# Modulated projection input by two VectorE operations around one ScalarE cast, and group C's attention low parts on GpSimd

## The chip, the cores and the metric

The kernel runs on one core of one Trainium2 chip. The metric is the device time of one execution in microseconds (us). TensorE multiplies matrices, VectorE and GpSimd do elementwise work, ScalarE activations and casts, and SyncE (SP) issues the DMAs.

## The reference

Two layers of a latent-diffusion trunk, on 512 latent tokens and 256 context tokens of width 1024. Each layer normalizes and modulates its input, projects it, lets three head groups attend, gates them, projects back and adds the residual:

```
sh, sc, gt = split(silu(c) @ w_ada[l] + b_ada[l], 3)
h  = rms_norm(x, norm_g[l]) * (1 + sc) + sh            # hc for the context tokens alike
qa, ka, va, ga, qb, kb, vb, gb, qn, kn, vn, gn = split_proj(h @ w_in[l])
# A: differential attention with rotary, B: grouped-query attention with rotary,
# C: 8 x 16 neighbourhood attention with a learned bias; each also attends to the context
y  = concatenate([ya, yb, yn]) @ w_out[l]              # each group gated by silu of ga, gb, gn
x  = x + gt * y                                        # the context likewise in the first layer
```

The first step's `rms_norm(...) * (1 + sc) + sh` is what the change touches: with rs the reciprocal root mean square of a token, mA = norm_g (1 + sc) and mB = sh, it is h = x rs mA + mB.

## The kernel before

Tokens lie along the free dimension: a tile of x is 128 features by 512 latents (`bigL`) or by 256 context tokens (`bigC`), and there are 8 feature tiles (kt 0 to 7). Products that need fp32 accuracy are made from two parts, hi (a value cast to fp32r) and lo (the value less its hi), by three matmuls: xh whi (L685), xh wlo (L686), xl whi (L687). `build_h` makes hi and lo of h for one kt and one stream. It is called 32 times, 8 kt by 2 streams by 2 layers:

- L431, VectorE: xn = x rs (rs is broadcast over partitions in the tile `stB`). xn is a tile of a ring of three (`p32`, printed as p).
- L432, VectorE: xn = xn mA + mB, with mA and mB as one number per partition.
- L434, ScalarE: hi = cast of xn.
- L435: lo = xn - hi, on VectorE for kt 0, 3 and 6, on GpSimd for the others.

In layer 0, `proj_first` takes kt after kt for all six token tiles of the first weight chunk (6 x 3 matmuls of 384 columns per kt), and before each kt it calls `ada_pair`, which makes mA and mB of that kt: matmuls with the modulation weights (L198) into a PSUM tile of a ring of two, a VectorE copy (L201), a summing matmul (L203), and two small VectorE operations that write mA (L208) and mB (L211). The layer's constants (`layer_consts`, L310 to L382, many tiny VectorE and GpSimd operations) are made in the same stretch. The weights' own low parts (`wlo`, L85) are made on GpSimd ahead of that stage and on VectorE during the first chunks. In layer 1 the context's h is built first, behind the sums of squares over the new x (L1190, summed by matmuls L400), then the latents' h.

The order of the instructions on each engine is planned at build time, from priorities and a model of the engines' times; each engine then runs its list in order.

In attention, a unit is one head by 128 queries: scores (L781), maximum (L836, or L833 with the bias table of group C), ScalarE exponential (L850) into a tile of the same `p32` ring, a cast to fp16 hi (L870), the low part p - hi (L871), a DMA that transposes both (L873), and the value matmuls (L906, L907). The engine of L871 is chosen by a table of shares,

```python
VSHARE = {"HA": (0, 1), "H": (0, 1), "G": (1, 1), "T": (1, 4), "HC": (1, 8), ...}
```

where "H" is the low part, the letter behind it the group, and (a, b) gives VectorE a of every b. Group A and B give all to GpSimd; group C gives every eighth to VectorE.

Of the kernel before, what the change touches and what calls it, by code (L numbers as in the profile page):

```python
# [10 lines left out]
F32 = mybir.dt.float32  # L11
# [4 lines left out]
AF = mybir.ActivationFunctionType  # L16
ALU = mybir.AluOpType
# [17 lines left out]

REST = {"C": 7}
AK = [[6, 2, 0, 2], [0, 1, 0, 2]]
VSHARE = {"HA": (0, 1), "H": (0, 1), "G": (1, 1), "T": (1, 4), "HC": (1, 8), "WB": (1, 2), "WC": (1, 1),
          "W1": (1, 1)}

class Share:
# [5 lines left out]
    def __call__(self, kind):  # L47
        a, b = VSHARE.get(kind + self.phase, VSHARE.get(kind, (0, 1)))
        i = self.n[kind] = self.n.get(kind, -1) + 1
        return self.nc.vector if i * a % b < a else self.nc.gpsimd  # L50
# [59 lines left out]
def tile_hybrid_block(ctx: ExitStack, tc: tile.TileContext, xT_d, cT_d, ng_d, w_ada, bT_d, w_in, w_out,  # L110
# [7 lines left out]
    V, A, G, PE, SP = nc.vector, nc.scalar, nc.gpsimd, nc.tensor, nc.sync  # L118
# [3 lines left out]
    def sb(shape, dt=F32, tag="", bufs=1):  # L122
        return pool.tile(shape, dt, tag=tag, bufs=bufs, name=tag)
# [38 lines left out]
    def big(s, dt=F32, shape=None):  # L162
        return sb(shape or [128, KT, SW[s]], dt, "bigL" if s == 0 else "bigC", 3)
# [247 lines left out]
    def norm_both():  # L411
        acc = nbuf["t"][:, 0:NT]
        rs = nbuf["t"][:, NT:2 * NT]
        ps = psV.tile([128, 512], F32, tag="pv", name="ssq")
        for j in range(6):
            PE.matmul(ps[:, j:j + 1], lhsT=acc[:, 128 * j:128 * j + 128], rhs=colD, start=True, stop=True)
        r = rsqrt(ps[:, 0:6], 6, 1.0, EPS)
        for st_, js in ((0, range(4)), (1, range(4, 6))):
            ps = psP.tile([128, 512], F32, tag="p", name="rsb")
            for i, j in enumerate(js):  # L420
                PE.matmul(ps[:, 128 * i:128 * i + 128], lhsT=r[:, j:j + 1].to_broadcast([128, 128]), rhs=ident,
                          start=True, stop=True)
            A.copy(out=rs[:, 128 * js[0]:128 * js[-1] + 128], in_=ps[:, 0:128 * len(js)])
        return rs[:, 0:NL], rs[:, NL:NT]

    def build_h(l, st_, kt, x, rs):
        mA, mB, _ = mods[l]
        w = SW[st_]
        hi, lo = hT[st_]
        xn = sb([128, NT], F32, "p32", 3)[:, 0:w]  # L430
        V.tensor_tensor(out=xn, in0=x[:, kt, :], in1=rs, op=ALU.mult)  # L431
        V.tensor_scalar(out=xn, in0=xn, scalar1=mA[:, kt, st_:st_ + 1], scalar2=mB[:, kt, st_:st_ + 1], op0=ALU.mult,  # L432
                        op1=ALU.add)
        A.copy(out=hi[:, kt, :], in_=xn)  # L434
        (V if kt % 3 == 0 else G).tensor_tensor(out=lo[:, kt, :], in0=xn, in1=hi[:, kt, :].bitcast(F32),  # L435
                                                 op=ALU.subtract)


    NH = {"A": 8, "B": 6, "C": 6}
# [759 lines left out]
    if True:  # L1199
        cT = sb([128, KT, 2], F32, "cT")  # L1200
        SP.dma_start(out=cT, in_=cT_d)
        x = [big(0), big(1)]
# [29 lines left out]
        rs = norm_both()  # L1232
# [3 lines left out]
        def before0(gi, kt):  # L1236
            if kt:
                ada_pair(ada0[kt])
            for st_ in range(2):
                build_h(0, st_, kt, x[st_], rs[st_])  # L1240
            if kt == 5:
                layer_consts(0)
# [7 lines left out]
        for l in range(DEPTH):  # L1250
# [14 lines left out]
            x = [big(0), big(1)]  # L1265
            open_norm()
            rs = [None, None]
# [6 lines left out]
            for kt in range(KT):  # L1274
                prio(-800)(build_h)(l + 1, 1, kt, x[1], rs[1])

            def before1(gi, kt):
                if gi == 1:
                    if kt == 0:
                        rs[0] = norm_finish(0)  # L1280
                        hT[0] = (big(0, F32R), big(0, F32R))
                    prio(-800)(build_h)(1, 0, kt, x[0], rs[0])
# [79 lines left out]
```

## Time and profile before

| | before |
|---|---|
| runs, median of 3 (lowest to highest) | 934.97 us (934.93 to 936.88) |
| the profiled execution | 930.04 us |
| its span in the profile | 928.2 us |
| mean granted TensorE clock | 0.95 |
| busy share: TensorE, VectorE, ScalarE, GpSimd | 89%, 74%, 64%, 58% |
| L431, L432, both streams, 64 instructions | 45.1 us busy |
| L434, 32 instructions | 15.9 us busy |
| L435, 20 on GpSimd, 12 on VectorE | 23.8 us on GpSimd |
| L871, 138 on GpSimd, 6 on VectorE | 204.2 us and 6.3 us |

Busy times are sums over instructions of the profiled execution; successive VectorE instructions overlap by under 0.1 us, so that sums are a little high. "PE" is TensorE's matmul, "PEld" its weight load, "DVE" VectorE, "ACT" ScalarE, "POOL" GpSimd, "SPq" the DMA issue of SyncE. A row of the timeline is start, duration, engine, line, operation, output and inputs, shape; in brackets stands how long the engine was idle before and what released it.

### The profile page before, as it was taken

The numbers are of one execution on the slowest core, as the hardware profiler recorded it, in microseconds if no ns is written. First come the engines' busy times: TensorE is split into PE (matmuls) and PEld (weight loads), VectorE is DVE, ScalarE is ACT, GpSimd is POOL, SyncE is SP. The second block draws the span as 40 slices with busy tenths as digits, with TensorE's granted clock in tenths as the row PEclk, the third lists the DMA queues.
The fourth block names the chain that finished last, engine by engine and source line by source line (L and its number), as shares of the span: only waits on it lengthen the run. The fifth ranks groups of instructions, "written<-read, shape, count | busy, mean of one in ns | idle before, by whom it ended". The sixth has DMA issues, their size and how long they took to land.

```text
span 928.2 us, 17966 instructions
## 1 busy us (share of the span) xinstructions
PE 829.5 (89%) x6386; PEld 709.7 (76%) x6386; DVE 682.7 (74%) x1306; ACT 592.3 (64%) x1269; POOL 541.3 (58%) x502
## 2 busy tenths in 40 slices
PE   5899997997998999797999989989959999988978
PEld 3788886786887889685777889878849888866757
DVE  5975788988678866467765797789877975855853
ACT  5334577885887687476563445478758978757740
POOL 2638846998798465432441047939988776732420
PEclk9899999998999999899999999999979999987979
DMA  9925895644979997989898713884556889995642
GB/s 307 331 90 135 204 215 133 154 85 127 194 156 221 195 221 170 227 213 229 183 234 235 243 61 101 184 189 101 140 132 156 168 188 249 240 253 134 134 114 83
DMA packets 361449, 165.47 MB, mean 178 GB/s; under 512 B 256656, under 2 KB 355216, under 8 KB 361104
## 3 DMA queue, kind: packets, MB, share of 16 engines
q1 hardware_dynamic: 361360, 164.33, 73.9%
q8 instruction: 50, 0.82, 0.4%
q14 instruction: 39, 0.32, 0.1%
HBM read 86.55 MB, written 15.47 MB: 110 GB/s over the span
## 4 chain that ended last, share of the span: by engine, by line
PE 46%; DVE 15%; DMA 13%; POOL 9%; issue 8%; ACT 7%; SPq 1%; DVEq 0%; POOLq 0%; ACTq 0%
PE proj L685 7%; PE proj L687 7%; PE proj L686 6%; PE sc L781 5%; DMA pt<-hl 4%; PE pv L906 3%; PE op L1093 3%; PE op L1094 3%; PE op L1095 2%; ACT p L850 2%; DVE mx L836 2%; DMA raw<-in_w_in_dram 2%; DMA stB<-in_btab_dram 2%; POOL hl L871 2%; POOL wlo L85 1%
## 5 line engine op out<-in xcount | busy, mean ns | idle before, releaser
L871 POOL TENSOR_TENSOR hl<-p,hl 128x768 f16<-128x768 f32 (+3 forms) x138 | 204.2, 1484 | 179.7 <-ACT hl L870 139.7
L685 PE MATMUL proj<-whi,bigL 128*128 128x384 f32 (+1 forms) x592 | 203.4, 344 | 9.8 <-DVE tb L608 3.8
L686 PE MATMUL proj<-wlo,bigL 128*128 128x384 f32 (+1 forms) x592 | 200.3, 338 | 0.9 <-POOL wlo L85 0.7
L687 PE MATMUL proj<-whi,bigL 128*128 128x384 f32 (+1 forms) x592 | 197.7, 336 | 0.0
L850 ACT ACTIVATE p<-sc,nb,gsc 128x768 f32<-128x768 f32 (+3 forms) x200 | 166.0, 844 | 14.3 <-DVE p L866 5.0
L836 DVE TENSOR_REDUCE mx<-sc 128x1 f32<-128x768 f32 (+2 forms) x128 | 118.7, 931 | 31.7 <-PE sc L781 31.2
L685 PEld LDWEIGHTS proj<-whi,bigL 128*128 128x128 f32 x592 | 115.4, 195 | 19.9 <-DVE tb L608 5.4
L870 ACT CAST hl<-p 128x768 f16<-128x768 f32 (+3 forms) x144 | 103.7, 725 | 33.0 <-DMA pt<-hl 18.5
L686 PEld LDWEIGHTS proj<-wlo,bigL 128*128 128x128 f32 x592 | 115.5, 195 | 3.9 <-POOL wlo L85 1.6
L687 PEld LDWEIGHTS proj<-whi,bigL 128*128 128x128 f32 x592 | 114.4, 194 | 3.3 <-issue 2.4
L85 POOL TENSOR_TENSOR wlo<-raw,whi 128x768 fp32r<-128x768 f32 (+1 forms) x44 | 82.9, 1893 | 30.0 <-ACT whi L82 24.8
L82 ACT CAST whi<-raw 128x768 fp32r<-128x768 f32 (+1 forms) x104 | 80.3, 779 | 30.8 <-DMA raw<-in_w_in_dram 16.2
L906 PEld LDWEIGHTS <-pt 128*128 128x128 f16 x736 | 65.9, 99 | 41.2 <-DMA pt<-hl 25.7
L85 DVE TENSOR_TENSOR wlo<-raw,whi 128x768 fp32r<-128x768 f32 (+1 forms) x60 | 65.2, 1090 | 25.3 <-ACT whi L82 22.5
L685 PE MATMUL proj<-whi,bigC 128*128 128x384 f32 (+2 forms) x224 | 75.8, 339 | 0.8 <-ACT xn L468 0.8
L686 PE MATMUL proj<-wlo,bigC 128*128 128x384 f32 (+2 forms) x224 | 74.8, 334 | 0.0
L687 PE MATMUL proj<-whi,bigC 128*128 128x384 f32 (+2 forms) x224 | 74.6, 335 | 0.0
L156 POOL TENSOR_TENSOR rsqb<-rsqb,half 128x12 f32<-128x12 f32 (+2 forms) x25 | 68.2, 2726 | 10.5 <-DVE rsqb L155 8.4
L907 PEld LDWEIGHTS <-pt 128*128 128x128 f16 x736 | 66.6, 100 | 4.2 <-issue 1.2
L906 PE MATMUL pv<-vA,pt 128*128 128x128 f16 (+2 forms) x424 | 52.2, 229 | 13.6 <-DMA pt<-hl 13.0
L838 ACT ACTIVATE nb<-mx,lnp,gsc 128x1 f32<-128x1 f32 (+1 forms) x104 | 39.6, 385 | 37.6 <-DVE mx L836 26.5
L781 PE MATMUL sc<-bigL 128*128 128x512 f16 (+4 forms) x184 | 46.1, 310 | 17.3 <-ACT p L850 16.7
(320 smaller groups left out, 2042.2 us busy)
## 6 DMA issues: line engine op xcount, KB each, us to landing
raw<-in_w_in_dram SPq DMA_DIRECT2D x56, 384.0 KB, 4.1
adw<-in_w_ada_dram SPq DMA_DIRECT2D x68, 256.0 KB, 3.8
raw<-in_w_in_dram SPq DMA_DIRECT2D x24, 256.0 KB, 3.6
raw<-in_w_out_dram SPq DMA_DIRECT2D x16, 384.0 KB, 4.0
g_d<-tb SPq DMA_DIRECT2D x20, 192.0 KB, 2.6
gt<-g_d SPq DMA_DIRECT2D x18, 192.0 KB, 2.9
hl<-in_w_ada_dram SPq DMA_DIRECT2D x12, 256.0 KB, 5.0
pt<-in_w_ada_dram SPq DMA_DIRECT2D x12, 256.0 KB, 5.2
```

The lines of the kernel that those rows point to most:

```text
L82: self.nc.scalar.copy(out=hi, in_=raw2)
L85: self.share("W").tensor_tensor(out=lo, in0=raw2, in1=hi.bitcast(F32), op=ALU.subtract)
L156: G.tensor_tensor(out=y, in0=x, in1=half[:, 0:n], op=ALU.pow)
L685: PE.matmul(ps, lhsT=xh, rhs=hi, start=(kt == 0), stop=False)
L686: PE.matmul(ps, lhsT=xh, rhs=lo, start=False, stop=False)
L687: PE.matmul(ps, lhsT=xl, rhs=hi, start=False, stop=(kt == KT - 1))
L781: PE.matmul(ps, lhsT=q, rhs=k, start=n == 0, stop=n == b[2] - 1)
L836: V.tensor_reduce(out=mx[:, 0:ns], in_=ps[:, 0:w * ns].rearrange("p (a b) -> p a b", b=w), axis=AX.X, op=ALU.max)
L850: A.activation(out=p[:, w * x:w * x + w], in_=u["ps", i][:, w * x:w * x + w], func=AF.Exp, bias=u["nb", i][:, x:x + 1], scale=lc[l]["sc"][ ...
L870: A.copy(out=hl[:, 0:n], in_=p)
L871: lo_eng.tensor_tensor(out=hl[:, n:2 * n], in0=p, in1=hl[:, 0:n], op=ALU.subtract)
L906: PE.matmul(po[r, :], lhsT=pt[:, b, r], rhs=V_[:, vt, c0:129], start=first, stop=False)
```

## The change

`build_h` does L431 and L432's work by one VectorE scalar_tensor_tensor, xn = x mA rs, without the shift. The ScalarE cast becomes an Identity activation with mB as its bias, so that hi = cast of (xn + mB). The low part is a second scalar_tensor_tensor, lo = (xn + mB) - hi, on VectorE for every kt. In the table of shares the entry "HC" goes, so that group C's L871 falls under "H" and is on GpSimd always.

```diff
-VSHARE = {"HA": (0, 1), "H": (0, 1), "G": (1, 1), "T": (1, 4), "HC": (1, 8), "WB": (1, 2), "WC": (1, 1),
+VSHARE = {"HA": (0, 1), "H": (0, 1), "G": (1, 1), "T": (1, 4), "WB": (1, 2), "WC": (1, 1),
           "W1": (1, 1)}
...
         xn = sb([128, NT], F32, "p32", 3)[:, 0:w]
-        V.tensor_tensor(out=xn, in0=x[:, kt, :], in1=rs, op=ALU.mult)
-        V.tensor_scalar(out=xn, in0=xn, scalar1=mA[:, kt, st_:st_ + 1], scalar2=mB[:, kt, st_:st_ + 1], op0=ALU.mult,
-                        op1=ALU.add)
-        A.copy(out=hi[:, kt, :], in_=xn)
-        (V if kt % 3 == 0 else G).tensor_tensor(out=lo[:, kt, :], in0=xn, in1=hi[:, kt, :].bitcast(F32),
-                                                 op=ALU.subtract)
+        V.scalar_tensor_tensor(out=xn, in0=x[:, kt, :], scalar=mA[:, kt, st_:st_ + 1], in1=rs, op0=ALU.mult,
+                               op1=ALU.mult)
+        b = mB[:, kt, st_:st_ + 1]
+        A.activation(out=hi[:, kt, :], in_=xn, func=AF.Identity, bias=b)
+        V.scalar_tensor_tensor(out=lo[:, kt, :], in0=xn, scalar=b, in1=hi[:, kt, :].bitcast(F32), op0=ALU.add,
+                               op1=ALU.subtract)
```

## The prediction

> **What bounds the kernel now.** I read the first and fourth parts of the page, then the table by stretches over the two places where the input is built, then the single instructions there. TensorE is busy 89% of the span, VectorE 74%, GpSimd 58%.
>
> ```profile
> span 928.2 us, 17966 instructions
> ...
> PE 829.5 (89%) x6386; PEld 709.7 (76%) x6386; DVE 682.7 (74%) x1306; ACT 592.3 (64%) x1269; POOL 541.3 (58%) x502
> ```
>
> `build_h` runs only between about 20 and 65 us (layer 0) and between 535 and 565 us (layer 1). In the table by stretches the columns are TensorE, its weight load, VectorE, ScalarE and GpSimd (busy us, instructions), the granted clock, the DMA share and GB/s:
>
> ```profile
> 20.00:30.00 10.00, 8.75 (x84) 6.76 (x77) 10.00 (x16) 4.52 (x11) 5.78 (x4) 0.83 1.12 337
> 30.00:40.00 10.00, 7.43 (x86) 6.12 (x85) 9.35 (x44) 2.81 (x9) 7.52 (x15) 0.85 1.10 327
> 40.00:50.00 10.00, 10.00 (x94) 8.66 (x94) 9.96 (x19) 3.73 (x9) 4.27 (x3) 0.98 1.04 311
> ...
> 540.00:550.00 10.00, 10.00 (x66) 9.39 (x64) 9.09 (x18) 4.28 (x11) 4.74 (x6) 0.89 0.00 0
> 550.00:560.00 10.00, 10.00 (x66) 9.85 (x58) 9.96 (x16) 5.03 (x13) 6.34 (x6) 1.00 0.19 54
> ```
>
> VectorE is full in all of these, and TensorE is full in three of the five. So a relief of VectorE is paid only where TensorE stands still or is slow; these places are the terms of the sum. They are, after the VectorE row that releases the first:
>
> ```profile
> 36.56 0.21 DVE L211 TENSOR_SCALAR mB<-ada,bT 128x2 f32<-128x2 f32 x1
> 36.87 0.56 PE L198 MATMUL ada<-hl,cS 128*32 128x128 f32 x8 [2.57 <-issue]
> 39.13 0.52 PE L686 MATMUL proj<-wlo,bigL 128*128 128x384 f32 x1
> 39.45 0.52 PE L685 MATMUL proj<-whi,bigL 128*128 128x384 f32 x1
> ...
> 60.31 0.44 PE L685 MATMUL proj<-whi,bigL 128*128 128x384 f32 x1 [0.78 <-ACT bigL L434]
> 60.59 0.34 PE L686 MATMUL proj<-wlo,bigL 128*128 128x384 f32 x1
> 60.76 0.34 PE L685 MATMUL proj<-whi,bigL 128*128 128x384 f32 x1
> ...
> 537.18 1.05 PE L400 MATMUL ssq<-colD,stB 128*128 128x1 f32 x8 [3.64 <-DVE stB L1190]
> 564.60 0.44 PE L687 MATMUL projs<-whi,bigL 128*128 128x384 f32 x1 [0.66 <-POOL bigL L435]
> ```
>
> After the 2.57 us gap a 384-column matmul starts every 0.32 us (39.13 to 39.45); after the 0.78 us gap, every 0.17 us (60.59 to 60.76). A long gap is thus paid a second time in a halved clock, a short one is not.
>
> **The change part by part.** Per call `build_h` had a VectorE multiply by rs (L431), a VectorE scale-and-shift (L432), a ScalarE cast (L434) and a subtraction (L435), on VectorE for kt 0, 3 and 6 and on GpSimd for the other five. Now it has two VectorE scalar_tensor_tensor around a ScalarE Identity with a bias. There are 8 calls per stream and layer, 32 in all. The durations (min/median/max, ns):
>
> ```profile
> L431 DVE TENSOR_TENSOR p<-bigL,stB x16: 675/687/2247, 19.8 to 560.4; 128x512 f32<-128x512 f32 x16
> L431 DVE TENSOR_TENSOR p<-bigC,stB x16: 410/420/2051, 20.5 to 543.2; 128x256 f32<-128x256 f32 x16
> ...
> L432 DVE TENSOR_SCALAR p<-p,mA,mB x32: 393/539/1750, 21.4 to 561.7; 128x512 f32<-128x512 f32 x16, 128x256 f32<-128x256 f32 x16
> ...
> L435 POOL TENSOR_TENSOR bigL<-p,bigL x10: 1291/1454/2242, 26.0 to 564.5; 128x512 fp32r<-128x512 f32 x10
> L435 POOL TENSOR_TENSOR bigC<-p,bigC x10: 731/744/982, 29.5 to 545.2; 128x256 fp32r<-128x256 f32 x10
> L435 DVE TENSOR_TENSOR bigL<-p,bigL x6: 675/680/689, 24.2 to 561.1; 128x512 fp32r<-128x512 f32 x6
> L435 DVE TENSOR_TENSOR bigC<-p,bigC x6: 410/419/426, 25.2 to 544.6; 128x256 fp32r<-128x256 f32 x6
> ```
>
> L432's row mixes the sizes: I read its median 539 as the undisturbed 512-wide pass and its minimum 393 as the 256-wide one. The new instruction at these sizes stands elsewhere in the kernel, with one input from PSUM; it will cost between L431's 0.687 and 0.420, which reads two SBUF tensors too, and these rows, which I take because the operation is the same:
>
> ```profile
> L1136 DVE SCALAR_TENSOR_TENSOR bigC<-op,mG,hl x4: 481/484/484, 509.0 to 515.7; 128x256 f32<-128x256 f32 x4
> L1136 DVE SCALAR_TENSOR_TENSOR bigL<-op,mG,pt x4: 745/748/751, 517.8 to 531.7; 128x512 f32<-128x512 f32 x4
> ```
>
> VectorE, undisturbed, per kt with both streams: before 0.687 + 0.420 for L431, 0.54 + 0.39 for L432, and in three of eight cases 0.680 + 0.419: 2.04 + 0.41 = 2.45 us on average. After: 2 x (0.748 + 0.484) = 2.46 us. VectorE's own work does not move: the change trades a cheap pass for the return of the GpSimd share. GpSimd loses 10 x 1.454 + 10 x 0.744 = 22 us of medians, all off the end's path except where it is named below.
>
> What moves is that GpSimd leaves the build. Its instruction stretches the VectorE one beside it:
>
> ```profile
> 26.03 1.71 POOL L435 TENSOR_TENSOR bigL<-p,bigL 128x512 fp32r<-128x512 f32 x1 [2.25 <-ACT bigL L434]
> 26.50 1.39 DVE L432 TENSOR_SCALAR p<-p,mA,mB 128x256 f32<-128x256 f32 x1
> ```
>
> The 256-wide L432 took 1.39 us, ending just after the GpSimd one at 27.74; its minimum is 0.393, so it lost 1.0 us. The new instructions read two SBUF tensors as L431 does, whose maximum of 2051 to 2247 ns shows that it suffers alike; so they will be stretched by what stays on GpSimd (the weight splits of L85), but not by L435. The Trainium skill (GPSIMD Engine Reference, Specifications) says that GpSimd shares its SBUF interfaces with VectorE and collides with instructions in a two-port mode or with two SBUF inputs; by that rule old and new forms are equally exposed, and the trace agrees (1.39 against 0.393 us).
>
> Term A, the 2.57 us gap. The third pair's shift (L211) was written at 36.56 to 36.77, and TensorE's next modulation matmuls, which reuse that PSUM tile, followed at 36.87. VectorE worked without a hole from 19.85 to there, so what it sheds ahead of this point closes the gap. kt 0 (whose subtraction was on VectorE): 3.14 to 2.46, -0.7. kt 1: 2.04 to 2.46, +0.4. The stretch at 26.50: -1.0. kt 2's two multiplications (0.687 + 0.420) could run ahead of their modulation factors; the new form multiplies by mA first and cannot, so -1.1 here. Together -2.4. I count 2.0 of the 2.57 and half of the clock's second price. That price: 8 matmuls at 0.32 instead of 0.17 are 1.2 us, of which 0.6. Bounds of A: a loss of 1.2, if the order on VectorE leaves the layer constants ahead of L211 and adds kt 1's two low parts (0.748 + 0.484), and a gain of 2.57 + 1.2 = 3.8.
>
> Term B, the 0.78 us gap at 60.31. One kt earlier the multiplication had to wait for a buffer of xn (a ring of three), held by a GpSimd subtraction:
>
> ```profile
> 57.29 0.94 DVE L431 TENSOR_TENSOR p<-bigC,stB 128x256 f32<-128x256 f32 x1 [0.86 <-POOL bigL L435]
> ```
>
> With the subtraction at 0.748 on VectorE right behind the cast, it comes free some 1.3 us earlier: gain 0.7 (bounds 0 and 0.8). Term C, 537.18: the first hi of layer 1 needs one VectorE pass of 0.484 instead of 0.420 + 0.393, 0.33 sooner, and the passes around the last sums of squares become fewer: 0.7 (bounds 0 and 2.0; the gap is mostly the last sum of squares itself). Term D, 564.60: the GpSimd low part was late; gain 0.6 (bounds 0 and 0.66). Behind 538 us TensorE is full, so the rest of layer 1's build is worth nothing: 30 us of TensorE cover it, and if that cover went, VectorE's 2.46 us per kt would still be under the 6 x 3 matmuls x 0.17 = 3.1 us of a kt.
>
> ScalarE: the cast gains a bias read from memory.
>
> ```profile
> L434 ACT CAST bigL<-p 128x512 fp32r<-128x512 f32 x16 | 9.6, 619 | 24.5 <-DVE p L432 24.4
> ...
> L850 ACT ACTIVATE p<-sc,nb,gsc 128x512 f32<-128x512 f32 x36 | 26.8, 770 | 4.8 <-DVE hl L871 2.8 <-POOL hl L871 1.7
> ```
>
> A 512-wide activation with two such operands takes 770 against 619 ns, so one costs between 0 and 0.15; I take 0.08. It is on the path at terms A to C only: -0.2 in all (bounds 0 and -0.4). The Trainium skill (ScalarE: Activation LUTs, What ACT_TABLE_LOAD costs) gives about 93 ns per pointer operand; by that the loss would be 0.3 and the sum 0.1 us smaller. It is a rule against the change.
>
> Group C's low parts: six of L871 go from VectorE to GpSimd. Near the end all three units of a burst are then in one queue:
>
> ```profile
> 883.49 2.34 POOL L871 TENSOR_TENSOR hl<-p,hl 128x512 f16<-128x512 f32 x2 [3.82 <-ACT hl L870]
> 884.98 1.40 DVE L871 TENSOR_TENSOR hl<-p,hl 128x512 f16<-128x512 f32 x1
> 886.41 0.67 ACT L850 ACTIVATE p<-sc,nb,gsc 128x384 f32<-128x384 f32 x1 [0.23 <-DVE hl L871]
> ```
>
> On GpSimd the third ends at 883.49 + 3 x 1.17 = 887.0 instead of 886.4, and the exponential waits for its buffer: +0.6 us; VectorE is free 1.4 us sooner for the next score maximum, which is not late. The other five lie beside output-projection matmuls; all six on the path at 0.55 each would be +3.3, and VectorE's 1.4 us freed at the end, if they count, -1.4. Taken: -0.5, as at the end. No DMA and no queue of SP changes in number; each transposed load of a moved unit is issued up to 0.6 us later.
>
> Sum: 2.6 + 0.7 + 0.7 + 0.6 - 0.2 - 0.5 = 3.9 us. The profiled execution took 930.04 us (928.2 span and 1.8 around it) and would take 926.1; the median of the runs is 934.97, 4.9 above it, so I forecast 934.97 - 3.9 = 931.1.
>
> **Rivals.** (1) Slower: the first pass now needs mA, so nothing of a kt can run ahead of its modulation matmuls. Place: layer 0, kt 1 to 7. After mA comes a 0.748 pass and a 0.70 cast instead of 0.54 and 0.62: 0.29 us per kt, 2.0 us; and with both low parts in VectorE's queue (1.23 us) in front of the next pair's copy and factors, five kts more would lose up to 6.2. With 60% of that, the tail's 0.5 and only terms C and D on the other side: 2.0 + 3.7 + 0.5 - 1.3 = 4.9 us, 939.9. It decides once TensorE waits over 0.7 us for hi or for the factors in five of the seven kts. For it: VectorE at 10.00, 9.35, 9.96 of 10 there. Against: TensorE at 10.00 between 40 and 50 us, fed from behind by low parts of the kt before.
>
> (2) No change: the instructions' order is planned anew at build time from modelled durations, and L211 again stands behind the constants; A and C are 0, B and D stay, the tail and the bias cost 0.6: 934.97 - 1.3 + 0.6 = 934.3.
>
> (3) Slower by the tail: GpSimd's bursts put all six moved parts on the path, +3.3, the bias 0.2, and A and C bring nothing: 934.97 + 3.5 - 1.3 = 937.2. For it: L850 waits for the VectorE part already (0.23 above). Against: five of the six have matmuls of the output projection beside them.
>
> (4) More than forecast: A entire (3.8), B and D entire, C 2.0 and the clock after its 3.64 us gap (another 1.2), the tail unharmed: 8.5 us, 926.5. For it: a gap of 0.78 us leaves the clock alone, so closing most of a gap saves its second price whole. Against: it asks for four places at once.
>
> **How the numbers follow.** Mine (929 to 933) 0.43, rival 4 0.14, rival 2 0.21, rival 1 0.14, rival 3 0.08. Faster and slower are counted from 0.2%, 1.9 us, about what runs of this kernel can tell from no change: faster 0.57, same 0.21, slower 0.22. The range reaches from half way beyond rival 4, 925.5, to just short of rival 1's value, 938.5; mine alone is 929 to 933.
>
> **What would show it.** L435 absent from GpSimd and no VectorE pass of the build over 1.2 us except beside L85; both passes near 0.74 and 0.48; the gap before TensorE's fifth pair of modulation matmuls under 1 us and 384-column matmuls behind it at 0.17; no gap at the last low part of layer 1. Wrong would be: that gap as long or longer, new waits of L685 for hi in layer 0, or a longer wait of L850 for GpSimd in group C.

## The result and the profile after

The changed kernel takes 943.96 us (median of 4 runs, 942.55 to 946.70) against 934.95 for the kernel before in the same comparison: ratio 1.0099, 95% interval 1.0071 to 1.0128. A second comparison of 12 runs (`e18` below) gave 942.89 us, ratio 1.0059 (1.0031 to 1.0087). The change makes the kernel slower by 0.6 to 1.0%; 931.1 was forecast. The ratios are taken between runs made side by side and need not be the quotients of the medians. The profiled execution took 943.91 us. Its page begins:

```profile
span 942.1 us, 17913 instructions
...
PE 829.7 (88%) x6386; PEld 712.5 (76%) x6386; DVE 667.8 (71%) x1288; ACT 594.7 (63%) x1269; POOL 528.2 (56%) x488
```

TensorE's work is the same (829.5 before), VectorE and GpSimd have less, and the span is 13.9 us longer. The build's instructions, all shapes and durations (min/median/max in ns, first and last start):

```profile
L431 DVE SCALAR_TENSOR_TENSOR p<-bigL,mA,stB x16: 737/746/1217, 20.0 to 560.8; 128x512 f32<-128x512 f32 x16
L431 DVE SCALAR_TENSOR_TENSOR p<-bigC,mA,stB x16: 471/481/2059, 20.7 to 540.7; 128x256 f32<-128x256 f32 x16
L434 ACT ACTIVATE bigL<-p,mB x16: 708/722/727, 20.8 to 562.6; 128x512 fp32r<-128x512 f32 x16
L435 DVE SCALAR_TENSOR_TENSOR bigL<-p,mB,bigL x16: 735/744/752, 21.5 to 564.2; 128x512 fp32r<-128x512 f32 x16
L435 DVE SCALAR_TENSOR_TENSOR bigC<-p,mB,bigC x16: 463/480/2047, 22.2 to 541.9; 128x256 fp32r<-128x256 f32 x16
```

They cost what the prediction took (0.748 and 0.484). The time is lost elsewhere. Five landmarks by their last start, first in before and then in after: the residual of layer 0 (that layer's end), the values of group B (`vB`), group A's gated output (L934), the values of group C (`vnc`), the last residual (L1171). The first start in the first row is the first evacuation of layer 0.

```profile
L592 DVE SCALAR_TENSOR_TENSOR vA<-proj,vna,vA x16: 338/346/353, 69.2 to 595.4; 128x128 f16<-128x128 f32 x16
L1136 DVE SCALAR_TENSOR_TENSOR bigL<-op,mG,hl x4: 745/748/751, 519.9 to 533.6; 128x512 f32<-128x512 f32 x4
L592 DVE SCALAR_TENSOR_TENSOR vB<-proj,vnb,vB x12: 334/340/353, 147.2 to 644.6; 128x128 f16<-128x128 f32 x12
L934 DVE TENSOR_TENSOR o<-o,gt x10: 402/484/1568, 165.0 to 756.2; 128x256 f32<-128x256 f32 x10
L592 DVE SCALAR_TENSOR_TENSOR vA<-proj,vnc,vA x12: 604/618/621, 296.9 to 773.5; 128x384 f16<-128x384 f32 x12
L1171 DVE SCALAR_TENSOR_TENSOR tA<-ot,mG,bigC x8: 342/344/351, 919.7 to 924.5; 128x128 f32<-128x128 f32 x8
```

```profile
L592 DVE SCALAR_TENSOR_TENSOR vA<-proj,vna,vA x16: 337/352/355, 66.7 to 598.5; 128x128 f16<-128x128 f32 x16
L1136 DVE SCALAR_TENSOR_TENSOR bigL<-op,mG,hl x4: 743/748/751, 519.4 to 533.1; 128x512 f32<-128x512 f32 x4
L592 DVE SCALAR_TENSOR_TENSOR vB<-proj,vnb,vB x12: 334/342/349, 144.1 to 646.5; 128x128 f16<-128x128 f32 x12
L934 DVE TENSOR_TENSOR o<-o,gt x10: 407/424/1673, 166.4 to 773.2; 128x256 f32<-128x256 f32 x10
L592 DVE SCALAR_TENSOR_TENSOR vA<-proj,vnc,vA x12: 587/616/621, 284.2 to 791.4; 128x384 f16<-128x384 f32 x12
L1171 DVE SCALAR_TENSOR_TENSOR tA<-ot,mG,bigC x8: 341/344/351, 933.6 to 938.4; 128x128 f32<-128x128 f32 x8
```

After is 2.5 us ahead at the first evacuation (69.2 to 66.7), 0.5 ahead at the end of layer 0, 1.9 late with group B's values, 17.0 late with group A's output (756.2 to 773.2) and 13.9 late at the end. So the loss lies in layer 1, and most of it shows between 645 and 773 us, behind the last instruction of the build (564.2). TensorE by stretches of layer 1, before and then after (stretch, its length, TensorE's busy us and instructions, granted clock, DMA share, GB/s):

```profile
560.00:640.00 80.00, 73.27 (x618) 1.00 0.66 149
640.00:680.00 40.00, 32.18 (x212) 0.94 0.53 133
680.00:700.00 20.00, 15.14 (x98) 0.78 0.67 167
700.00:726.00 26.00, 26.00 (x186) 1.00 0.57 143
726.00:780.00 54.00, 51.67 (x402) 1.00 0.97 205
...
560.00:780.00 220.00, 198.26 (x1511) 0.97 0.70 161
```

```profile
560.00:640.00 80.00, 74.08 (x574) 0.96 0.63 138
640.00:680.00 40.00, 35.93 (x253) 1.00 0.62 133
680.00:700.00 20.00, 9.90 (x47) 0.57 0.52 97
700.00:726.00 26.00, 22.00 (x165) 1.00 0.69 169
726.00:780.00 54.00, 51.23 (x366) 0.94 0.74 150
...
560.00:780.00 220.00, 193.15 (x1398) 0.93 0.65 140
```

Over the whole stretch after works on 1398 TensorE instructions, before on 1511; the rest it has to do later. The deepest place is 680 to 700 us, where TensorE is busy 9.90 us of 20 at a clock of 0.57. Neither edit touches an instruction there: it is group A's softmax beside projections of later chunks. What differs is the order. Of the 2520 TensorE instructions of layer 1 that both kernels have, 1944 stand at another place in the list, by up to 125 places.

### The profile page after: what moved, and what is told of

It is laid out like the page before. It is cut to its first block, busy times and chain, and to the rows that moved or that the text cites. A ratio compares the mean times of both kernels' runs of the same rounds, so it can differ in the third digit from the quotient of the medians.

```text
span 942.1 us, 17913 instructions
## 1 busy us (share of the span) xinstructions
PE 829.7 (88%) x6386; PEld 712.5 (76%) x6386; DVE 667.8 (71%) x1288; ACT 594.7 (63%) x1269; POOL 528.2 (56%) x488
## 5 line engine op out<-in xcount | busy, mean ns | idle before, releaser
L871 POOL TENSOR_TENSOR hl<-p,hl 128x768 f16<-128x768 f32 (+3 forms) x144 | 212.6, 1483 | 184.4 <-ACT hl L870 155.8
L685 PE MATMUL proj<-whi,bigL 128*128 128x384 f32 (+1 forms) x592 | 206.0, 348 | 15.6 <-DVE tb L608 4.4
L687 PE MATMUL proj<-whi,bigL 128*128 128x384 f32 (+1 forms) x592 | 199.8, 340 | 0.0
L850 ACT ACTIVATE p<-sc,nb,gsc 128x768 f32<-128x768 f32 (+3 forms) x200 | 166.3, 844 | 19.7 <-DVE p L866 14.0
L685 PEld LDWEIGHTS proj<-whi,bigL 128*128 128x128 f32 x592 | 117.5, 198 | 24.5 <-DVE tb L608 5.6
L686 PEld LDWEIGHTS proj<-wlo,bigL 128*128 128x128 f32 x592 | 117.8, 199 | 3.6 <-issue 1.5
L687 PEld LDWEIGHTS proj<-whi,bigL 128*128 128x128 f32 x592 | 116.5, 197 | 2.8 <-issue 1.2
L906 PEld LDWEIGHTS <-pt 128*128 128x128 f16 x736 | 66.1, 100 | 44.4 <-DMA pt<-hl 30.2
L685 PE MATMUL proj<-whi,bigC 128*128 128x384 f32 (+2 forms) x224 | 75.7, 338 | 4.2 <-ACT bigC L434 2.4
L85 DVE TENSOR_TENSOR wlo<-raw,whi 128x768 fp32r<-128x768 f32 (+1 forms) x60 | 62.1, 1040 | 20.9 <-ACT whi L82 17.7
L907 PEld LDWEIGHTS <-pt 128*128 128x128 f16 x736 | 66.7, 101 | 3.8 <-issue 1.2
L781 PE MATMUL sc<-bigL 128*128 128x512 f16 (+4 forms) x184 | 47.8, 319 | 19.5 <-ACT p L850 19.2
L906 PE MATMUL pv<-vA,pt 128*128 128x128 f16 (+2 forms) x424 | 52.5, 231 | 13.0 <-DMA pt<-hl 12.8
```

The lines of the kernel that those rows point to most:

```text
L85: self.share("W").tensor_tensor(out=lo, in0=raw2, in1=hi.bitcast(F32), op=ALU.subtract)
L685: PE.matmul(ps, lhsT=xh, rhs=hi, start=(kt == 0), stop=False)
L686: PE.matmul(ps, lhsT=xh, rhs=lo, start=False, stop=False)
L687: PE.matmul(ps, lhsT=xl, rhs=hi, start=False, stop=(kt == KT - 1))
L850: A.activation(out=p[:, w * x:w * x + w], in_=u["ps", i][:, w * x:w * x + w], func=AF.Exp, bias=u["nb", i][:, x:x + 1], scale=lc[l]["sc"][ ...
L871: lo_eng.tensor_tensor(out=hl[:, n:2 * n], in0=p, in1=hl[:, 0:n], op=ALU.subtract)
```

## The experiments

The order can be held. Each kernel's list for each engine is taken from its build, and another kernel is built with edges between successive instructions of that list, edges that carry no semaphore and only bind the planner. Instructions that the list lacks (the 20 low parts that change engine in the build, the six of group C) find their own place. As a sketch:

```diff
+    for engine, numbers in ORDER.items():      # the other kernel's list, by the order of the source
+        last = None
+        for i in (have[n] for n in numbers if n in have and have[n].engine == engine):
+            if last is not None:
+                tc.add_manual_dep(i, last.name, NoSync, reason="order")
+            last = i
```

After bound to its own list (`e18`) runs the same instructions in the same order as unbound, so the binding itself adds nothing. Every ratio is against runs of before beside it on the same chip, with its 95% interval; the median of before itself lay between 933.7 and 936.3 us in these comparisons, so the ratios are to be compared and not the times. In the expectations, the theories are that the order costs the time, that the new instructions do, and that group C's move does.

**Instructions against order.** `e1_new_ops_old_order`: all of after's instructions in before's order.

> The changed kernel's instructions, but every instruction that both kernels have on the same engine stands in the order that the kernel before has (the 20 build low parts that come over from GpSimd and the six low parts of group C are the only ones placed freely). Theory O (the newly planned order costs the time, the instructions themselves do not): 928 to 936 us, no slower than before. Theory I (the instructions cost it: everything of the build in VectorE's queue and nothing that runs ahead of its factors): 941 to 947, as the changed kernel. Theory T (six low parts of group C on GpSimd): 938 to 944.

928.81 us, ratio 0.9953 (0.9927 to 0.9979): faster than before, by 4.4 us if the ratio is taken. `e2_old_ops_new_order`: before's instructions in after's order.

> The kernel before's instructions in the changed kernel's order. Theory O: 942 to 950 us, as slow as the changed kernel or slower. Theory I: 933 to 938. Theory T: 933 to 938, since its six parts are back on VectorE.

948.25 us, ratio 1.0137 (1.0095 to 1.0179). The order alone costs 1.4%; the instructions alone gain 0.5%.

**Each edit alone, planned anew and in the old order.** `e3_build_only` keeps "HC": (1, 8) in the table of shares; `e4_groupC_only` keeps the old `build_h`.

> The build's edit alone; group C's shares stay as before; the order is planned anew. Theory I: 941 to 946. Theory T: 930 to 936. Theory O says nothing of the sign, only that the time can lie anywhere from 928 to 950, since this is a third order.

> The shares' edit alone: six low parts of group C on GpSimd, the build as before; planned anew. Theory T: 938 to 944 (its waits near the end of each layer). Theory I: 934 to 936. Theory O: again a new order, 928 to 950, and where it is slow the loss lies also in groups A and B, which the edit does not touch.

942.61 us, 1.0118 (1.0074 to 1.0162), and 942.96 us, 1.0093 (1.0063 to 1.0124): either edit alone, once planned anew, loses as much as both. In the old order:

> The build's edit alone, group C's shares as before, in the order of the kernel before (only the 20 build low parts that come over from GpSimd are placed freely). If the order is what cost the time and my terms A to D are right: 926 to 932 us. If the six low parts of group C matter by themselves (I took 0.5, at most 3.3 us), this lies below both edits in the old order (928.8) by that much; if they do not, the two agree within 1.5 us. If the build's edit is worth nothing by itself: 934.

> The shares' edit alone, the build as before, in the order of the kernel before (the six moved low parts are placed freely on GpSimd). Order alone is the cause: 932 to 936 us, against 943.0 for the same edit planned anew. The moved parts are the cause: 938 or more.

929.58 us, 0.9944 (0.9917 to 0.9971), and 933.83 us, 1.0002 (0.9978 to 1.0026). The build's edit is worth half a per cent; group C's, which as planned costs 0.9%, is itself worth nothing that can be measured.

**Which layer's order.** The changed kernel with the old order in layer 1 only (`e7`), and in layer 0 only (`e8`).

> The changed kernel with the old order held for the instructions of layer 1 alone; layer 0 is planned freely, as in the changed kernel. The changed kernel's trace is 0.5 us ahead at the end of layer 0 and 14 us late at the end of layer 1. If the loss is in layer 1's order: 928 to 934 us. If it comes from what layer 0's order leaves behind: 940 or more.

> The changed kernel with the old order held for layer 0 alone; layer 1 is planned freely. If the loss is in layer 1's order: 938 to 950 us, since layer 1 gets a fresh plan behind another layer 0. If layer 0's order is what costs: 928 to 934.

932.37 us, 0.9984 (0.9959 to 1.0009), and 943.98 us, 1.0098 (1.0073 to 1.0123): the loss is in layer 1's order. That `e7` lies above `e1` leaves room for some 0.3% in layer 0's new order, which the intervals don't separate.

**Is it this change, or any new plan?** One number of the kernel before is changed, so that 5, 2 or 4 of the 144 low parts of L871 are on VectorE instead of 6.

```diff
-... "HC": (1, 8), ...
+... "HC": (1, 9), ...      # e9;  (1, 16) in e10;  (1, 12) in e14
```

> The kernel before with one number changed: group C's share is one in nine, so 5 of the 144 low parts of L871 are on VectorE and not 6; the order is planned anew (1619 of layer 1's 2520 TensorE instructions stand elsewhere, by up to 138 places). Moving all six in the old order cost nothing, so moving one is worth under 0.1%. Theory G (the order of before is an unusually good one, and any new plan of this kernel loses what it gains): 939 to 946. Theory S (plans scatter, and after drew a bad one): anything from 928 to 945, as often under as over 937. Theory E (only the build's new instructions and the whole move of group C lead to a bad plan): 934, within 0.3% of before.

> As the run with one in nine, with one in sixteen: 2 of 144 low parts on VectorE, and a third plan (1083 TensorE instructions of layer 1 moved, by up to 79 places). Theory G: 939 to 946. Theory S: 928 to 945, and apart from the other by some 5 us. Theory E: 934.

943.44 us, 1.0121 (1.0087 to 1.0156), and 933.05 us, 0.9991 (0.9963 to 1.0019). By `e6` even six moved parts cost under 0.3% in the old order; one gives a plan that is 1.2% slower, four a plan as good as before. So a slow plan belongs neither to this change nor to every new plan: plans scatter by over 1%. With `e14` (below) there are six kernels planned wholly anew (after, `e3`, `e4`, `e9`, `e10`, `e14`): five are slower than before by 0.6 to 1.2%, one is as fast, none is faster. The order of before lies at the good end of the scatter; why it does, no run here shows.

**Which half of layer 1.** The changed kernel with the old order held up to, or from, the 84th L906 of layer 1 (726 us in before).

> The changed kernel, with the old order held in the first half of layer 1 alone (to the 84th value matmul of L906 in that layer, at 726 us in the profile of before); layer 0 and the second half are planned anew. Theory F (the new plan spends its projection matmuls before 680 us, has none to put beside group A's softmax between 680 and 720, and so loses the time there): 930 to 934, and TensorE busy over 33 us between 660 and 700 less than 24 no more. Theory H (the loss is in the second half, where group C's values come 18 us late): 941 to 945. If each half bears its part: 936 to 940.

> The changed kernel, with the old order held from that 84th value matmul on alone; layer 0 and the first half of layer 1 are planned anew. Theory F: 940 to 945, with TensorE busy about 10 of 20 us between 680 and 700. Theory H: 930 to 934. If each half bears its part: 936 to 940.

934.67 us, 1.0010 (0.9988 to 1.0031), and 940.27 us, 1.0066 (1.0040 to 1.0093). The first half's order carries the loss; holding the second half gives nothing back against `e18`. The two are a clean pair: in the traces `e12` has after's own lists up to the place where the held part begins, and `e11`'s TensorE list is that of before to 851 us. (`e11` lies just above the range of theory F, at 934.67 against 934.) The expectation's figure for TensorE between 660 and 700 us was misread (33 us): before has 29.06 there, `e11` 28.35. The two between 680 and 726 us, `e11` and then `e12`:

```profile
680.00:700.00 20.00, 12.79 (x67) 0.66 0.73 125
700.00:726.00 26.00, 25.46 (x172) 0.93 0.58 146
```

```profile
680.00:700.00 20.00, 9.74 (x58) 0.66 0.51 96
700.00:726.00 26.00, 21.08 (x148) 0.95 0.68 168
```

The same landmarks as above, as differences (us), one profiled execution each:

| kernel | end of layer 0 | from there to B's values | from there to A's output | from there to the end of the span |
|---|---|---|---|---|
| before | 533.6 | 111.0 | 111.6 | 172.0 |
| `e1` old order | 531.7 | 109.9 | 111.8 | 169.4 |
| `e10` 1 in 16 | 532.1 | 111.1 | 113.4 | 170.5 |
| `e11` first half | 533.2 | 113.7 | 115.3 | 174.7 |
| after | 533.1 | 113.4 | 126.7 | 168.9 |
| `e18` after again | 535.3 | 114.6 | 126.6 | 168.9 |
| `e12` second half | 533.4 | 112.9 | 123.0 | 169.4 |
| `e3` build only | 536.5 | 109.3 | 122.9 | 170.0 |
| `e4` group C only | 538.0 | 112.6 | 119.4 | 171.1 |
| `e9` 1 in 9 | 541.4 | 114.7 | 121.3 | 163.1 |
| `e14` 1 in 12 (below) | 537.4 | 114.6 | 116.6 | 173.1 |

Every slow plan needs more for one stretch, from group B's values to group A's last output: 117 to 127 us where the good ones need 112 to 115. (The others fit: 125.6 in `e2` and 124.3 in `e8`; 112.6 in `e5`, 111.5 in `e6`, 115.4 in `e7`.) It is least in `e14`, which like `e3`, `e4` and `e9` ends layer 0 late as well, by 3 to 8 us. That lateness tells nothing of a plan: `e6`, as fast as before, ended layer 0 at 542.2 in its profiled execution, and after and `e18`, the same lists, differ by 2.2 us there and by 0.1 in the stretch. TensorE in the stretch, before and then after (columns as above):

```profile
644.60:756.20 111.60, 97.05 (x665) 0.94 0.66 153
```

```profile
646.50:773.20 126.70, 105.77 (x712) 0.91 0.64 146
```

Not all of the 15.1 us more is idleness. After has 47 more TensorE instructions in the stretch, which before has in the stretches on both sides, and is busy for 8.7 us more; it is idle for 20.9 us against 14.6. By this idle time the slow plans part from the good ones in every profiled execution: 17.7 to 22.8 us in the thirteen slow kernels (`e13` and `e15` to `e18` below among them), 13.5 to 16.8 in the seven good ones.

A sign seemed to go with the time. Between 560 and 680 us, and between 680 and 700, before starts 189 and 18 of the projections L685, after 198 and 7, `e9` 197 and 9: the slow ones do their projections early and have few beside group A's softmax. A further plan was made to see whether the sign can fail:

> The kernel before with group C's share at one in twelve: 4 of the 144 low parts on VectorE; a further plan of nearly the same instructions (1554 TensorE instructions of layer 1 stand elsewhere, by up to 79 places). Theory S (plans scatter): 928 to 945, the place not to be told beforehand. Theory F adds a sign: at 940 or above, TensorE starts at least 197 matmuls of L685 between 560 and 680 us and at most 9 between 680 and 700; at 936 or below, at most 192 and at least 12. Against F: a time on one side with the counts of the other.

942.84 us, 1.0078 (1.0050 to 1.0106), with 200 and 8, as foretold. Yet the test was worth little: fixed stretches also count how late layer 0 ended (537.4 in `e14`). Moved so that each begins as far behind the end of layer 0 as in before, they give 192 and 12 for `e14` and 189 and 11 for `e9`, against 193 and 12 for `e11`, which is not slow. For after (199 and 7) the sign stays, but it does not part the slow plans from the others.

**Is that place the cause?** In the trace of after no projection starts between 678.83 and 694.08 us (rows of the timeline; in brackets the idle time and its releaser):

```profile
678.83 0.34 PE L687 MATMUL proj<-whi,bigL 128*128 128x384 f32 x1
681.70 0.58 PE L781 MATMUL sc<-bigL 128*128 128x512 f16 x1 [2.52 <-ACT p L850]
...
685.30 0.58 PE L781 MATMUL sc<-bigL 128*128 128x512 f16 x1 [2.81 <-ACT p L850]
...
688.71 0.29 PE L906 MATMUL pv<-vA,pt 128*128 128x128 f16 x1 [2.61 <-DMA pt<-hl]
...
693.63 0.59 PE L781 MATMUL sc<-bigL 128*128 128x512 f16 x1 [2.44 <-ACT p L850]
...
694.08 0.67 PE L685 MATMUL proj<-whi,bigL 128*128 128x384 f32 x1
```

`e13` moves 20 projection matmuls from behind this hole into it and lets the other lists follow (TensorE's list; S is one unit's scores, V one unit's values, P a projection matmul):

```diff
-S     S     V S     S 20P
+S  6P S  6P V S 3P  S  5P
```

> The changed kernel with after's own TensorE order in layer 1, but for one move: 20 projection matmuls that stood behind four units of group A's softmax (from 694.08 us in the profile of after) are put between these units, where TensorE stood still from 679 to 694 us. The other engines' lists follow from that (39 VectorE and 40 ScalarE instructions move, by up to 9 places). Theory F (TensorE without other work in that hole is a cost of the new plan): 20 x 0.17 = 3.4 us, and up to 3.2 more for the halved clock behind the hole: 937 to 941. If the softmax units themselves set the time there and the hole is only where TensorE waits for them: 943 to 945. If the units become later because the matmuls stand in front of their scores: over 945.

941.75 us, 1.0052 (1.0025 to 1.0080), between the ranges of the theories and not told apart from after's 1.0059 to 1.0099: little if anything, and the trace says why.

```profile
695.37 0.69 PE L685 MATMUL proj<-whi,bigL 128*128 128x384 f32 x1 [9.07 <-DVE tb L608]
```

They wait 9.07 us for VectorE's L608, the last reader of the PSUM tile that they need. In after it runs at 693.12 although its tanh was done at 683.17. `e15` puts L608 five places ahead on VectorE and the 20 matmuls behind the second and third unit; `e16` moves L608 alone.

```diff
 TensorE, e15
-S S     V S    S 20P
+S S 11P V S 9P S
 VectorE, e15 and e16
-L522      L864 L836 L866 L836 L504 L608
+L522 L608 L864 L836 L866 L836 L504
```

> The changed kernel with all of after's own order in layer 1 but for two moves. On VectorE, the L608 of one gate chunk, which in after ran at 693.12 us though its tanh (L606) was done at 683.17, stands five places further ahead, behind the L522 of 683.40. On TensorE, the 20 projection matmuls that wait for that L608 to free their PSUM tile (in the run before, where they alone were moved, for 9.07 us) stand between the second and the fourth of the four softmax units. Theory R (the new order puts L608 behind the maxima of later units, so that projections and softmax follow each other where they could lie side by side): the hole from 679 to 694 us shrinks by 20 x 0.17 = 3.4 us, and the clock stays higher: 937 to 941. If the softmax alone paces this stretch and what is won here is waited for again before 780 us: 943 to 945.

> As the run with both moves, with VectorE's move alone: L608 five places ahead, TensorE's order that of after. Theory R: the release comes 9 us sooner, but the matmuls that need it still stand behind the four units: 943 to 944.5, as after. If the place of L608 alone is what matters: 938 to 941.

944.08 us, 1.0100 (1.0065 to 1.0134), and 941.83 us, 1.0070 (1.0039 to 1.0100): theory R fails in `e15`, `e16` lies between its two ranges, and neither is told apart from after. VectorE now stands waiting in front of L608, in `e16`:

```profile
687.75 0.55 DVE L608 SCALAR_TENSOR_TENSOR tb<-sq,proj 128x384 f32<-128x384 f32 x1 [5.76 <-POOL xn L496]
```

L608 writes a tile of a ring of two that GpSimd's L496 still reads, and L496 stands on GpSimd behind a weight split and a low part. `e17` has `e15`'s moves and this one; `e18` is the changed kernel itself beside it.

```diff
 GpSimd, e17
-L491 L493 L85  L929 L871 L496
+L491 L493 L496 L929 L871 L85
```

> The changed kernel in its own order of layer 1, but for three moves around one place. In the run with two moves, L608 waited 5.22 us on VectorE for GpSimd's L496, which frees the tile tb that L608 writes; in after this L496 stands on GpSimd behind a weight split (L85, 2.12 us), L929 and a low part (L871), and ran at 688.32 us. Here L496 and L871 stand ahead of that L85; L608 and the 20 projection matmuls stand as in the run with two moves. Theory R (the interlock of three lists at this place is the loss): the matmuls run while softmax does, 937 to 941, and TensorE is idle at no point between 680 and 700 us for over 2.6 us. If the loss is spread over the first half and this place is only where it is seen: 942 to 946, whatever the hole does.

> The changed kernel, instruction for instruction in its own order, beside the run with three moves on the same chip: 941 to 946 by every theory.

942.90 us, 1.0050 (1.0019 to 1.0081), and 942.89 us, 1.0059 (1.0031 to 1.0087). The interlock is undone: L608 waits for L496 for 0.89 us and not for 5.76 (it runs at 687.75 here too, but this execution had ended layer 0 2.8 us later than that of `e16`), and the projections run between the units, 11 behind the second and 9 behind the third. Nothing is gained against `e18`, as the theory of a spread loss had it. Waits come back behind them, for the transposed low parts:

```profile
688.50 0.67 PE L685 MATMUL proj<-whi,bigL 128*128 128x384 f32 x1
...
691.30 0.34 PE L686 MATMUL proj<-wlo,bigL 128*128 128x384 f32 x1
...
698.19 0.29 PE L906 MATMUL pv<-vA,pt 128*128 128x128 f16 x1 [2.42 <-DMA pt<-hl]
...
703.48 0.29 PE L906 MATMUL pv<-vA,pt 128*128 128x128 f16 x1 [2.06 <-DMA pt<-hl]
```

From group B's values to group A's output `e17` takes 124.5 us, `e18` 126.6, before 111.6. Shown is that the order of layer 1's first half carries the loss and that the loss appears between these two landmarks. The hole at 680 us is a part of it at most; which other moved instructions make the rest is left open.

## Why the prediction was wrong

**What held: the total of the sum, and not all of its make-up.** `e1` is the change as the prediction priced it, with the lists as they were. Its profiled execution is 5.4 us shorter than that of before (924.66 against 930.04), the ratio of the runs says 4.4 (interval 2.0 to 6.8), and the sum said 3.9. Lines of `e1` are 97 higher than in after, since the marks for the order stand ahead of them (L295 is L198, L497 is L400, L782 is L685).

```profile
35.42 0.42 PE L295 MATMUL ada<-hl,cS 128*32 128x128 f32 x8 [2.06 <-issue]
...
37.20 0.34 PE L783 MATMUL proj<-wlo,bigL 128*128 128x384 f32 x1
37.38 0.34 PE L782 MATMUL proj<-whi,bigL 128*128 128x384 f32 x1
...
534.67 1.05 PE L497 MATMUL ssq<-colD,stB 128*128 128x1 f32 x8 [2.97 <-DVE stB L1287]
```

```profile
L689 DVE SCALAR_TENSOR_TENSOR vA<-proj,vna,vA x16: 340/346/356, 65.9 to 592.5; 128x128 f16<-128x128 f32 x16
```

- Terms A and B, 2.6 + 0.7: the first evacuation comes at 65.9 instead of 69.2, 3.3 us sooner, and at 67.2 in `e5`. One execution cannot settle so little: nine kernels whose lists of layer 0 are those of after have it anywhere from 66.7 (after) to 70.7 (`e13`). Of the 3.3 us, 1.9 are left at the end of layer 0 (531.7 against 533.6); the rest of the 5.4 comes in layer 1, where C and D were to bring 1.3. In `e5` the two shares are 2.5 and 1.0. So the total came near the forecast in part by luck, and it does not confirm the single terms.
- A's make-up was off. Its gap closed by 0.5 (2.57 to 2.06; 2.07 in `e5`) and not by 2.0, though it ended 1.45 us sooner. New gaps of 0.42 and 0.54 us stand behind it (36.92 and 52.95), for hi, of the kind that rival 1 names. B's gap is gone.
- The clock's second price, counted at half in A, is not a matter of the build. Before pays it behind this gap and `e1` does not, but `e5`, with the new build, pays it (a 384-column matmul starts every 0.32 us from 36.98), and `e6`, with the old build and a gap of 2.60 us, does not (every 0.17 us from 38.87). As far as these four executions tell, it was chance that before's paid it.
- Term C, 0.7: the gap at layer 1's first sums of squares is 2.97 instead of 3.64, in `e5` too. Term D, 0.6: no gap is left there. After's own plan loses both: TensorE waits there in four places between 535 and 552 us, for 5.6 us in all, and in before in two for 4.3.
- The bias: L434 takes 722 against 619 ns, 0.10 us and not 0.08. The Trainium skill (ScalarE: Activation LUTs, What ACT_TABLE_LOAD costs) gives about 93 ns per pointer operand; the trace is near it with 103.
- A reading: VectorE was called full in all five stretches; in two it was at 9.35 and 9.09 of 10.
- The tail, 0.5: `e6` bounds group C's move between a gain of 2.1 us and a loss of 2.4; the runs cannot tell it from 0.

**What failed: the sum was made over lists that the change does not leave in place.** Every term compares one instruction's start before and after with the same neighbours. The prediction had the planner in the lower bound of term A and in rival 2, both bounded to the build's own stage; in rival 2 the new plan could at worst bring nothing. What a new plan does to the instructions that no edit touches was put at nothing, without a reason. The runs showed, in its place, 1944 moved TensorE instructions in layer 1 and a loss of 1.4% from the new lists alone (`e2`), nearly three times what the edit brings. The cost of a new plan was taken to lie between nothing and the loss of the gain, and the range ended at 938.5.

**The signs were set at the wrong stage.** The waits named as what would show the steps wrong were those of the build in layer 0 and of L850 for GpSimd in group C. Neither came in after: L685 waits for hi in layer 0 twice, for 0.2 us each, and L850 for GpSimd 2.4 us in all, against 2.1 before. What grew is TensorE's wait for group A's softmax (L781 for L850), from group B's values to group A's output, before (644.6 to 756.2 us) and then after (646.5 to 773.2; total us, times, longest):

```profile
PE sc L781 <- ACT p L850: 4.8, 2, 3.9
```

```profile
PE sc L781 <- ACT p L850: 9.4, 5, 2.8
```

A total over the whole program would mislead here: L850's wait for VectorE's L866 grows from 5.0 to 14.0 us, but 11.1 of that lies ahead of 300 us, in layer 0, where after is not late.

**The rivals.** Rival 1 (the first pass needs mA, slower in layer 0) gave a time nearest to the result, 939.9, and is not its cause: `e5` has that pass and is 0.6% faster than before. Rival 2 named the right actor, the plan made anew, and the wrong size. Rival 3 (group C's tail) falls by `e6`. Rival 4's 8.5 us lie beyond the intervals of `e1` and `e5` (up to 6.8 and 7.8).

`e1` and `e5` are the better versions: 0.5 and 0.6% faster than before, so 1.1 to 1.5% faster than after, with the build's edit and the old order.

## What to carry to other kernels

Where a planner writes the order, an edit is two changes: its instructions, and a new list for every engine, far from the edit too. Here the first was worth -0.5% and the second up to +1.4%, and one low part moved to another engine gave +1.2%. An order that lies at the good end of the scatter, as the one before did, is more likely to be lost by a new plan than bettered (five of six here). Hold the old order to learn what an edit is worth, price the new plan by small edits that are worth nothing, and treat the plan as something to choose: a good edit is to be kept with the order that suits it.

## What the runs showed of the hardware

Whether the clock falls behind a gap of TensorE is not told by that gap's length, nor by the kernel. After and `e18` have the same instructions in the same lists, and TensorE waits 2.44 us in both at the start of layer 1. Behind it a matmul of 384 columns starts every 0.18 us in after (535.80 to 535.98) and every 0.32 us in `e18` (538.13 to 538.45):

```profile
535.52 0.45 PE L685 MATMUL proj<-whi,bigC 128*128 128x384 f32 x1 [2.44 <-ACT bigC L434]
535.80 0.34 PE L686 MATMUL proj<-wlo,bigC 128*128 128x384 f32 x1
```

```profile
537.68 0.65 PE L685 MATMUL proj<-whi,bigC 128*128 128x384 f32 x1 [2.44 <-ACT bigC L434]
538.13 0.53 PE L686 MATMUL proj<-wlo,bigC 128*128 128x384 f32 x1
```

So the prediction's reading, that a long gap is paid a second time in a halved clock, is no rule: it held behind the gap of 2.57 us in before, and not behind 2.60 us at the same place in `e6` nor behind 2.44 us in after. What decides it no run here shows.
